# One inference step of a two-layer hybrid trunk: the decode token moved to the second block, the second S5 set-up to the third, and the first retention mixer begun earlier

## The chip, the cores and the metric

The kernel runs on one core of one Trainium2 chip. The metric is the device time of one execution in microseconds (us). The core has five engines that run side by side and meet through semaphores: PE (matrix products; its weight loads are listed apart as PEld), DVE (vector work), ACT (activations, copies), POOL (vector work), and SP, which here only issues DMAs. Each engine works through its own list of instructions in order, so an instruction that waits holds up all that stand behind it on that engine.

## The reference, cut to what matters

A prompt of 2048 tokens and, apart from it, 8 single new tokens with carried states (the decode token below) go through two layers. Each layer is:

```
hn   = rms_norm(x) * norm_w
proj = hn @ w_in                  # 1024 -> 3332 columns
A: RetNet retention on rotated q, k           (4 heads of 64)
B: HGRN2 gated linear recurrence              (4 heads of 64)
C: S5 diagonal complex state space, then GLU  (16 groups, 64 states)
D: Mamba-2 SSD with a causal convolution      (4 heads of 64)
x    = x + concat(A, B, C, D) @ w_out
```

After the second layer a last rms_norm gives y_prompt and y_sample. The states after the prompt and after the decode token are outputs too. All is float32.

## The kernel before

The prompt is cut into four blocks of 512 tokens for each layer, so there are eight blocks, 0 to 3 in the first layer and 4 to 7 in the second. For each block the code runs projections on PE: `gemm_A` (columns of the retention), `gemm_H` (HGRN), `gemm_M` (Mamba) and `gemm_S` (S5), and one block later `out_proj`. Every product is made as three products of high and low parts of its operands; ACT (lines L607, L680) and DVE (L608, L681) split each weight tile first. In the trace the projections are L620, L625 and L687 (L687 with `mx` as its input is `out_proj`).

The work that is no projection is written as generators, the streams, and each `yield` is a place where others may step in. After each piece of a projection `tick()` lets at most two streams of the lanes m, s, a, h (the mixers of the block) and one of the lanes d, e, f, p (decode and set-up) make one step. So the order on PE is the order in which this code runs; the order on the other engines is made by a scheduler that takes the priorities (`SPRI`, `DPRI` and others) into account. `finish(B)` first drains all streams of block B, then runs its `out_proj`.

Three pieces of side work matter here:

- The decode token (class `Dec`). Its 8 rows ride along with the projections of one block of each layer: `dec_pass` multiplies the raw weight tile by them (L630, L694 on PE), `collect` adds the four partial sums (L779 on ACT, L781 on DVE). Its four small mixers (`mix_A`, `mix_H`, `mix_M`, `mix_S` of `Dec`) and `mix_all` are streams. Before, it goes with block 0 and with block 4. `split_T` (L800) turns its normed rows.
- The S5 set-up (`s5_setup`), once for each layer: on DVE powers of the complex decay (`cmul`, `exp_poly`, `sincos`), then tables that pass through HBM (`gpad`, `s5c`: L508, L512, L517, L518) and come back in the S5 mixer (L241, L1447, L1448). The first layer's begins at block 0; the second's, before, at the end of block 1.
- The mixers of a block. For blocks 1 to 7 the mixers A and H begin with the `out_proj` of the block ahead. For block 0 there is none, so before both begin after `gemm_H`, with waits of at most one tick (`most=1`).

Scratch comes from pools of tiles that are handed out again when free: `half` has 10 tiles of 512 columns, `big` 10 of 1024.

Of the kernel before, what the change touches and what calls it, by code (L numbers as in the profile page):

```python
# [113 lines left out]
def trunk_kernel(ctx: ExitStack, tc: tile.TileContext, A: dict):  # L114
# [229 lines left out]
    def sincos(sn, cn, hi, lo, shape):  # L344
        n = tmp_c(shape)
        r = tmp_c(shape)
# [19 lines left out]
    def s5_setup(L):  # L366
# [303 lines left out]
    def gemm_wide(lhs, w, c0, evac, dec=None):  # L670
# [4 lines left out]
        def load(kt):  # L675
            with tc.high_priority(offset=WPRI):
                hl = whp.tile([P, 2, 520], F32R, name=nm("wh"), tag="wh")
                raw = wrp.tile([P, 520], F32, name=nm("wr"), tag="wr")
                nc.sync.dma_start(raw[:, 0:512], w[kt * P : (kt + 1) * P, c0 : c0 + 512])
# [5 lines left out]
        def t_pass(kt, tt):  # L685
            for pi, (a, c) in enumerate(((1, 0), (0, 1), (0, 0))):
                T.matmul(banks[tt], lhs[kt][:, a, tt * P : (tt + 1) * P], hls[kt][:, c, 0:512],  # L687
                         start=(kt == 0 and pi == 0), stop=(kt == KT - 1 and pi == 2))

        def dec_pass(kt):  # L690
            if dec is not None and kt % DW == DW - 1:
                for k in range(kt - DW + 1, kt + 1):
                    j = k % 4
                    T.matmul(dbank[32 * j : 32 * j + 8, :], dec[0]()[:, k, :], raws[k][:, 0:512], start=(k < 4), stop=(k >= 4))  # L694
# [43 lines left out]
    class Blk:  # L738
# [3 lines left out]
        used = 0  # L742

        def free(self, kt):
            return lambda: self.prev is None or self.prev.used > kt
# [41 lines left out]
    class Dec:  # L787
# [209 lines left out]
        def mix_S(self):  # L997
            l, L = self.l, self.L
            gw = load_gw(L)
# [30 lines left out]
            y = half([P, 8, 2, 16])[0:8]  # L1030
# [11 lines left out]
            so = half([P, 2, P])[0:64]  # L1042
# [4 lines left out]
            db = half([P, 2, 256])[0:8]  # L1047
            us = half([P, 2, 256])[0:8]
            nc.sync.dma_start(us[:, 0], self.d["su"])
            nc.sync.dma_start(us[:, 1], self.d["sg"])  # L1050
            nc.sync.dma_start(db[:, 0], A["s5_D"][l].partition_broadcast(8))
            nc.sync.dma_start(db[:, 1], A["s5_glu_b"][l].partition_broadcast(8))
            V.tensor_tensor(db[:, 0], db[:, 0], us[:, 0], ALU.mult)
            V.tensor_tensor(yf, yf, db[:, 0], ALU.add)
# [6 lines left out]
            V.tensor_copy(gT, ps[:, 0:16].rearrange("p (k b) -> p k b", k=2))  # L1061
            yield 4
# [3 lines left out]
            V.tensor_tensor(db[:, 1], db[:, 1], ps[0:8, 0:256], ALU.add)  # L1066
            S.activation(db[:, 1], db[:, 1], AF.Sigmoid)
            V.tensor_tensor(yf, yf, db[:, 1], ALU.mult)
            V.tensor_tensor(yf, yf, us[:, 1], ALU.mult)
# [190 lines left out]
    def mix_H(L, B):  # L1260
# [17 lines left out]
        for l in range(7):  # L1278
            h = 1 << l
            nb = TB // (2 * h)  # L1280
            ntot = (half([P, 2, nb]) if l < 3 else small([P, 2, nb], f"h_t{l}", bufs=1))
# [372 lines left out]
    def out_proj(L, B, src, dst, last, parts=(0, 1)):  # L1654
        w = A["w_out"][L.l]
        fwb = [None, None]
        if last:
# [68 lines left out]
        if not final:  # L1726
            for hf in parts:
                for k, _ in enumerate(gemm_wide(B.mix, w, hf * 512, evac_wide(hf), dec=B.dec and B.dec.out(hf, last))):
                    if hf == 1:
                        B.used = k + 1 if k < 6 else (6 if k == 6 else 8)  # L1730
                    yield
        else:
            gens = []
            for hf in range(4):
                if hf % 2 == 0:
                    dec = B.dec and B.dec.out(hf // 2, last)
                gens.append(gemm(B.mix, w, hf * 256, "T", evac(hf), dec=dec, late=hf == 3))
# [5 lines left out]
            drain(B.st["m"])  # L1743
            for g in gens:
# [110 lines left out]
    for i in range(nblk):  # L1855
# [7 lines left out]
        B.hn, B.st = [], {}  # L1863
# [19 lines left out]
    def begin(ph, B):  # L1883
        B.st[ph] = spawn(ph, mixer(ph, B), most=1 if B.prev is None and ph in "ah" else 9)
# [121 lines left out]
```

## Time and profile before

| what | value |
|---|---|
| three timed runs | 2296.26, 2297.53, 2297.86 us; median 2297.53 |
| the profiled execution | 2296.06 us |
| its span, first to last instruction | 2294.3 us |
| PE busy | 2140.4 us (93%) |
| DVE busy | 1668.9 us (73%) |
| ACT busy | 1037.3 us (45%) |
| POOL busy | 236.4 us (10%) |
| mean granted clock of PE | 0.965 |

Busy time is time in which at least one instruction of the engine runs. A matrix product that runs while the granted clock is 0.5 takes longer and counts as busy for longer, so busy time on PE holds the time that a low clock costs. Rows of waits say which instruction of which line waited for which producer, with the total, the count and the longest.

### The profile page before, as it was taken

To read this page: it belongs to the slowest core of one execution; us is meant where nothing else is said; L and a number is where in the kernel's file an instruction comes from. 1 tells how busy PE (TensorE), PEld (TensorE's weight loads), DVE (VectorE), ACT (ScalarE), POOL (GpSimd) and SP (SyncE) were. 2 spreads that over 40 slices of the span, in tenths; PEclk is the share of its full clock that TensorE was granted. 3 is DMA by queue.
4 is the path that set the end of the run, shared out by engine and by line. 5 is a ranking of instruction groups with operands and counts; after the bars stand their busy time and mean duration, and the time that the engine had idled before them with its cause. 6 is when DMAs were issued, how large, how long until landed. Compare 5 with 4: busy or idle time off the path is not lost. (4 is left out here: it accounts for less than half of the span.)

```text
span 2294.3 us, 41082 instructions
## 1 busy us (share of the span) xinstructions
PE 2140.4 (93%) x15047; PEld 1732.4 (76%) x15047; DVE 1668.9 (73%) x4625; ACT 1037.3 (45%) x1893; POOL 236.4 (10%) x212
## 2 busy tenths in 40 slices
PE   7988898999999999999999999899999989999967
PEld 6767676778777887779777777676877778778856
DVE  6778885587957876397676798658875787647855
ACT  5334633346442464434543365334545345444423
POOL 1010102001022011101020000200101001110100
PEclk9998899999999999999999999999999999999988
DMA  6322466154533655243434246415454433533342
GB/s 190 91 58 71 155 167 155 50 147 127 168 101 109 159 161 165 68 138 87 146 116 134 82 134 180 145 61 177 116 159 122 127 105 100 163 87 109 121 134 84
DMA packets 265242, 284.94 MB, mean 124 GB/s; under 512 B 88848, under 2 KB 185760, under 8 KB 265040
## 3 DMA queue, kind: packets, MB, share of 16 engines
q1 hardware_dynamic: 265040, 282.31, 41.7%
q8 instruction: 118, 1.93, 0.3%
q14 instruction: 84, 0.69, 0.1%
HBM read 246.05 MB, written 31.99 MB: 121 GB/s over the span
## 5 line engine op out<-in xcount | busy, mean ns | idle before, releaser
L687 PE MATMUL gb<-wh,hn 128*128 128x512 f32 x2208 | 542.0, 401 | 3.7 <-DVE half L1626 3.6
L625 PE MATMUL gb<-hn,wh 128*128 128x512 f32 x1920 | 489.0, 408 | 7.0 <-DVE half L1118 7.0
L687 PEld LDWEIGHTS gb<-wh,hn 128*128 128x128 f32 x2208 | 411.3, 189 | 109.8 <-issue 13.8
L625 PEld LDWEIGHTS gb<-hn,wh 128*128 128x128 f32 x1920 | 361.7, 193 | 98.0 <-issue 11.9
L681 DVE TENSOR_TENSOR wh<-wr,wh 128x512 fp32r<-128x512 f32 x296 | 216.3, 735 | 273.2 <-ACT wh L680 271.7
L680 ACT CAST wh<-wr 128x512 fp32r<-128x512 f32 x296 | 183.4, 620 | 394.1 <-PE gb L687 193.4
L687 PE MATMUL gb<-wh,mx 128*128 128x512 f32 x1344 | 339.3, 405 | 7.4 <-DVE half L1700 6.9
L687 PEld LDWEIGHTS gb<-wh,mx 128*128 128x128 f32 x1344 | 250.0, 191 | 75.6 <-DVE half L1700 11.6
L607 ACT CAST wh<-wr 128x512 fp32r<-128x512 f32 (+1 forms) x248 | 152.2, 619 | 320.1 <-PE gb L625 95.9
L608 DVE TENSOR_TENSOR wh<-wr,wh 128x512 fp32r<-128x512 f32 (+1 forms) x248 | 183.2, 745 | 87.0 <-ACT wh L607 85.8
L620 PE MATMUL gb<-wh,hn 128*128 128x256 f32 (+1 forms) x1728 | 225.2, 291 | 2.1 <-DVE hn L556 1.1
L620 PEld LDWEIGHTS gb<-wh,hn 128*128 128x128 f32 x1728 | 217.6, 196 | 5.6 <-issue 2.6
L1561 POOL TENSOR_TENSOR half<-mats,m_lal 128x512 fp32r<-128x512 f32 x64 | 75.4, 1199 | 820.8 <-DVE m_lal L1555 311.0
L1317 DVE COPY_PREDICATED big<-lvl,mb 64x256 f32<-64x256 int32 x192 | 95.9, 538 | 2.7
L1284 ACT COPY zbH<-big 64x512 f32<-64x512 f32 x112 | 70.8, 632 | 46.7 <-PE mb L1293 39.4
L1499 DVE SCALAR_TENSOR_TENSOR big<-gb,vt,big 128x511 f32<-128x511 f32 (+2 forms) x96 | 71.1, 744 | 3.9 <-ACT big L1497 3.4
L1293 PE MATMUL mb<-zbH,big 128*64 128x64 f32 x1536 | 58.2, 232 | 5.2 <-ACT half L1165 3.5
L1293 PEld LDWEIGHTS mb<-zbH,big 128*64 128x64 f32 x1536 | 51.9, 145 | 14.5 <-issue 7.7
L1275 POOL TENSOR_TENSOR big<-mats,h_dg 128x1024 f32<-128x1024 f32 x16 | 30.6, 1932 | 282.3 <-DVE h_dg L1272 282.3
L1458 PE MATMUL mb<-big,big 128*64 128x128 f32 x512 | 40.7, 304 | 18.2 <-DMA big<-s5c 14.2
L620 PE MATMUL gb<-wh,mx 128*128 128x256 f32 x384 | 51.1, 298 | 4.6 <-DVE mx L1481 4.1
L620 PEld LDWEIGHTS gb<-wh,mx 128*128 128x128 f32 x384 | 50.0, 204 | 6.1 <-DVE mx L1481 4.9
(495 smaller groups left out, 3084.6 us busy)
## 6 DMA issues: line engine op xcount, KB each, us to landing
wr<-in_w_in SPq DMA_DIRECT2D x416, 256.0 KB
wr<-in_w_out SPq DMA_DIRECT2D x128, 256.0 KB
big<-s5c SPq DMA_DIRECT2D x64, 256.0 KB
xn<-xmid SPq DMA_DIRECT2D x32, 512.0 KB
xn<-in_x_prompt SPq DMA_DIRECT2D x24, 512.0 KB
big<-s5c SPq DMA_DIRECT2D x24, 512.0 KB
xmid<-half SPq DMA_DIRECT2D x44, 256.0 KB
half<-xmid SPq DMA_DIRECT2D x44, 256.0 KB
```

Of the source, the lines that this page charges most:

```text
L607: S.copy(hl[:, 0, :, :n], raw[:, :, :n])
L608: V.tensor_tensor(hl[:, 1, :, :n], raw[:, :, :n], hl[:, 0, :, :n].bitcast(F32), ALU.subtract)
L620: T.matmul(o, lhs[2 * ks[ki] + k][:, a, tt * P : (tt + 1) * P], hls[ki][:, c, k, :n], start=(ki == 0 and k == 0 and pi == 0 and tt % per = ...
L625: T.matmul(banks[i], hls[ki][:, a, k, i * P : (i + 1) * P], lhs[2 * ks[ki] + k][:, c, :], start=(ki == 0 and k == 0 and pi == 0), stop=(ki ...
L680: S.copy(hl[:, 0, 0:512], raw[:, 0:512])
L681: V.tensor_tensor(hl[:, 1, 0:512], raw[:, 0:512], hl[:, 0, 0:512].bitcast(F32), ALU.subtract)
L687: T.matmul(banks[tt], lhs[kt][:, a, tt * P : (tt + 1) * P], hls[kt][:, c, 0:512], start=(kt == 0 and pi == 0), stop=(kt == KT - 1 and pi = ...
L1284: S.copy(qz[sl, r, :].rearrange("p (b h) -> p b h", h=h), q[sl].rearrange("p a (b two h) -> p (a b) two h", two=2, h=h)[:, :, 1, :])
L1293: T.matmul(ps[su, j * 64 : (j + 1) * 64], k[:, j // 4, (j % 4) * P + 64 * u : (j % 4) * P + 64 * u + 64], qz[:, :, j * 64 + 32 * u : j * 6 ...
L1317: V.copy_predicated(stv[p][su, :, nu * u : nu * u + nu, :], mv, ps[su, p * 256 : p * 256 + 256].rearrange("p (c b h) -> p c b h", c=8, h=h))
L1499: V.scalar_tensor_tensor(acc[:, 3 - i :], ps[:, : TB - 3 + i], w(i), acc[:, 3 - i :], ALU.mult, ALU.add)
L1561: E('m').tensor_tensor(mms[tt][i].rearrange("p (h t) -> p h t", h=4), tri[:, None, :].to_broadcast([P, 4, P]), lal[:, i, tt, :][:, :, None ...
```

## The change

The decode token now goes with block 1 and block 5 (`if B.b == 0: nxt.dec = Dec(...)`), the set-up of the second layer waits until the decode token's S5 mixer is done and so runs in block 2, and block 0's retention mixer begins ahead of `gemm_H`, its HGRN mixer after it (waits of at most two ticks). Beside these the code needs fewer `half` tiles: `cmul` uses its outputs as scratch, several pairs of small tiles share one tile, the GLU weight of the decode token and the final norm weight are loaded later. `ks`, `B.order`, `B.used` and `tmp` are passed through with values that leave the old order of the products.

```diff
     def cmul(outr, outi, ar, ai, br, bi, shape, neg_i=False):
...
-        t1, t2 = tmp_c(shape), tmp_c(shape)
-        V.tensor_tensor(t1, ar, br, ALU.mult)
+        t2 = tmp_c(shape)
+        V.tensor_tensor(outr, ar, br, ALU.mult)
         e.tensor_tensor(t2, ai, bi, ALU.mult)
-        V.tensor_tensor(outr, t1, t2, ALU.subtract)
-        t3, t4 = tmp_c(shape), tmp_c(shape)
+        V.tensor_tensor(outr, outr, t2, ALU.subtract)
+        t3, t4 = outi, tmp_c(shape)
...
-            ctz = half([P, 2, 4, 2, 16])
-            gtile = half([P, 2, 8, 16])
+            cg = half()
+            ctz = cg[:, 0:256].rearrange("p (a q r c) -> p a q r c", a=2, q=4, r=2)
+            gtile = cg[:, 256:512].rearrange("p (z g c) -> p z g c", z=2, g=8)
...
+            if l == 0:
+                ntot = half([P, 2, nb])
+            elif l < 3:
+                if l == 1:
+                    t12 = half([P, 384])
+                ntot = (t12[:, 0:256] if l == 1 else t12[:, 256:384]).rearrange("p (a b) -> p a b", a=2)
...
     def begin(ph, B):
-        B.st[ph] = spawn(ph, mixer(ph, B), most=1 if B.prev is None and ph in "ah" else 9)
+        B.st[ph] = spawn(ph, mixer(ph, B), most=2 if B.prev is None and ph in "ah" else 9)
...
-        B.dec = Dec(layers[0], A["x_sample"].rearrange("b o d -> b (o d)"))
-        ll, dn, ga = load_layer(layers[0]), B.dec.norm(), gemm_A(B.L, B)
+        ll, ga = load_layer(layers[0]), gemm_A(B.L, B)
...
-        next(dn)
-        next(ga)
-        for _ in dn:
-            pass
+        load = setup = None
         setup = spawn("p", s5_setup(layers[0]), SPRI, "s")
...
             run(ga if i == 0 else gemm_A(B.L, B))
+            if B.prev is None:
+                begin("a", B)
             run(gemm_H(B.L, B))
             if B.prev is not None:
-                finish(B.prev, ("a", B), ("h", B), parts=(0, 1) if nxt is not None else (0,))
+                finish(B.prev, ("a", B), ("h", B))
             else:
-                begin("a", B)
                 begin("h", B)
...
+            if B.b == 0:
+                drain(load)
+                nxt.dec = Dec(B.L, B.prev.dec_dst if B.prev else A["x_sample"].rearrange("b o d -> b (o d)"))
+                prep = spawn("d", nxt.dec.norm(), DPRI, "d")
...
             if B.b == 1 and B.l + 1 < DEPTH:
-                    drain(setup)
-                    setup = spawn("p", then(load_layer(layers[B.l + 1]), s5_setup(layers[B.l + 1])), SPRI, "s")
+                load = spawn("p", load_layer(layers[B.l + 1]), SPRI, "s")
+                def after(B):
+                    yield lambda: B.st["ds"].done
+                    yield from s5_setup(layers[B.l + 1])
+                setup = spawn("p", after(B), SPRI, "s")
```

On PE, at block 0's retention mixer (L1163 turns q and k, L1173 scores, L1186 state, L1202 the part from the state; L1270 is the HGRN mixer's first product, L465 the set-up's), there stands before, within `gemm_M`:

```order
L1186 MATMUL mb_1560<-big_744,half_701 64x64 x4
L1202 MATMUL mb_1569<-hAb_111,half_1524 128x128 x2
L1163 MATMUL mb_1572<-mats,half_423 128x128 x2
L1163 MATMUL mb_1572<-mats,half_701 128x128 x2
L1270 MATMUL mb_1579<-mats,big_1527 128x2 x8
L465 MATMUL mb_1597<-s_dm_1462,mats 128x16
L625 MATMUL gb_1498<-hn_147,wh_1602 128x512 x3
```

and now, within `gemm_H`:

```order
L1186 MATMUL mb_1037<-big_652,half_627 64x64 x4
L1202 MATMUL mb_1046<-hAb_111,half_992 128x128 x2
L1163 MATMUL mb_1049<-mats,half_400 128x128 x2
L1163 MATMUL mb_1049<-mats,half_627 128x128 x2
L625 MATMUL gb_967<-hn_149,wh_1060 128x512 x3
L625 MATMUL gb_967<-hn_150,wh_1060 128x512 x3
L625 MATMUL gb_968<-hn_149,wh_1060 128x512 x3
```

The retention's steps moved one projection ahead, and the HGRN mixer's steps no longer stand between them.

On SP, the loads and stores of the first set-up's tables (`gpad` to `s5c`, L517 and L518) and the S5 mixer's loads of them (L1447, L1448) stand before among the loads of rotary tables (L1142) and weights:

```order
L517 DMA big_3423<-gpad_1601 128x8x16 x5
L1447 DMA big_3896<-s5c_2_129 128x512
L604 DMA wr_4099<-in_w_in 128x2x256
L1448 DMA big_3897<-s5c_4_131 128x512
L1142 DMA half_3823<-in_c_rot 128x512
L518 DMA s5c_3_130<-big_3423 128x1024
L1448 DMA big_3897<-s5c_5_132 128x512
L679 DMA wr_4141<-in_w_in 128x512
L1142 DMA half_3838<-in_c_rot 128x512
L1447 DMA big_3896<-s5c_3_130 128x512
```

and now:

```order
L512 DMA s5c_5_132<-big_2676 256x1x128 x4
L517 DMA big_2859<-gpad_1630 128x8x16 x8
L518 DMA s5c_2_129<-big_2859 128x1024
L679 DMA wr_3047<-in_w_in 128x512
L679 DMA wr_3052<-in_w_in 128x512
L679 DMA wr_3159<-in_w_in 128x512
L679 DMA wr_3199<-in_w_in 128x512
L517 DMA big_2869<-gpad_1630 128x8x16 x8
L518 DMA s5c_3_130<-big_2869 128x1024
```

The second store L518 now stands ten rows ahead of the first load of what these stores wrote; before it stood between those loads.

On PE, at the end of block 1's `gemm_M` and the start of its last projection (`gemm_S`'s second half, L625), there stands before:

```order
L620 MATMUL gb_5616<-wh_5740,hn_3008 128x256 x3
L1567 MATMUL mb_5785<-m_la_5667,mats 128x16 x3
L625 MATMUL gb_5799<-hn_2827,wh_5801 128x512 x3
L625 MATMUL gb_5800<-hn_2827,wh_5801 128x512 x3
L625 MATMUL gb_5799<-hn_2835,wh_5801 128x512 x3
L625 MATMUL gb_5800<-hn_2835,wh_5801 128x512 x3
L581 MATMUL mb_5818<-mats,xn_5775 128x128 x4
```

and now (L1574 is L1567 of before):

```order
L630 MATMUL mb_5238<-wr_5391,dT_1792 8x256 x2
L1574 MATMUL mb_5445<-m_la_5289,mats 128x16 x3
L898 MATMUL mb_5458<-half_5304,mats 128x64
L625 MATMUL gb_5467<-hn_2397,wh_5470 128x512 x3
L625 MATMUL gb_5468<-hn_2397,wh_5470 128x512 x3
L625 MATMUL gb_5467<-hn_2405,wh_5470 128x512 x3
L625 MATMUL gb_5468<-hn_2405,wh_5470 128x512 x3
L581 MATMUL mb_5487<-mats,xn_5435 128x128 x4
```

The decode token's products (L630, and L898 of its retention mixer) came into block 1, between products that stood there alone.

## Rows read from the trace of the kernel before

**Rows 1.** The page: busy time by engine, and the granted clock in 40 slices.

```profile
PE 2140.4 (93%) x15047; PEld 1732.4 (76%) x15047; DVE 1668.9 (73%) x4625; ACT 1037.3 (45%) x1893; POOL 236.4 (10%) x212
...
PEclk9998899999999999999999999999999999999988
```

**Rows 2.** Windows: stretch, its length, busy time by engine (instructions), PEclk, DMA share, GB/s.

```profile
0.00:78.00 78.00, 61.04 (x378) 51.56 (x378) 58.74 (x241) 37.88 (x86) 9.93 (x23) 0.96 0.51 156
78.00:129.00 51.00, 51.00 (x250) 36.85 (x247) 28.64 (x100) 22.45 (x44) 2.38 (x1) 1.00 0.33 99
129.00:278.00 149.00, 123.56 (x1044) 100.72 (x1042) 128.00 (x363) 68.74 (x116) 17.88 (x16) 0.87 0.30 89
278.00:346.00 68.00, 64.62 (x395) 50.67 (x394) 59.28 (x163) 28.89 (x64) 10.73 (x8) 0.95 0.63 171
346.00:417.00 71.00, 60.00 (x349) 45.36 (x347) 41.11 (x81) 30.72 (x50) 11.22 (x10) 0.93 0.48 124
417.00:491.00 74.00, 70.25 (x597) 53.37 (x596) 55.49 (x158) 24.83 (x44) 3.77 (x2) 1.00 0.34 104
491.00:766.00 275.00, 262.82 (x1818) 215.42 (x1818) 213.44 (x650) 124.72 (x222) 36.34 (x33) 0.98 0.44 128
766.00:1024.00 258.00, 253.09 (x1757) 207.95 (x1756) 177.57 (x470) 121.63 (x214) 26.67 (x22) 0.99 0.49 137
1024.00:1289.00 265.00, 261.98 (x1850) 207.47 (x1849) 191.17 (x482) 123.46 (x218) 25.57 (x25) 0.99 0.39 119
1289.00:1581.00 292.00, 275.28 (x1956) 214.57 (x1958) 225.94 (x594) 134.54 (x250) 25.91 (x21) 0.98 0.42 125
1581.00:1843.00 262.00, 252.66 (x1764) 206.83 (x1757) 188.96 (x508) 126.75 (x231) 26.22 (x21) 0.99 0.46 138
```

**Rows 3.** Timeline of PE around the decode token's first product: start, us, instruction [idle before].

```profile
33.72 1.02 PE L800 MATMUL mb<-mats,big 8*128 8x8 f32 x8 [4.49 <-DVE big L812]
34.67 5.20 PE L620 MATMUL gb<-wh,hn 128*128 128x256 f32 x24
```

**Rows 4.** Waits of PE from 129 to 278 us: total, times, longest.

```profile
PE mb L722 <- DVE half L736: 9.0, 2, 4.9
PE mb L1186 <- DVE big L1502: 3.9, 1, 3.9
PE mb L1173 <- DVE big L1317: 2.6, 1, 2.6
```

**Rows 5.** Waits of PE from 278 to 417 us.

```profile
PE mb L1458 <- DMA big<-s5c: 8.6, 3, 4.0
PE mb L1474 <- DMA half<-in_s_glu_w: 2.4, 1, 2.4
```

**Rows 6.** Groups of DVE from 129 to 278 us: count | busy us, mean ns | idle before.

```profile
L781 DVE TENSOR_TENSOR half<-half,mb 8x256 f32<-8x256 f32 (+2 forms) x18 | 8.3, 462 | 0.6
...
L1192 DVE SCALAR_TENSOR_TENSOR hAb<-hAb,mats,mb 64x64 f32<-64x64 f32 x16 | 4.5, 278 | 0.3
...
L859 DVE TENSOR_TENSOR half<-half,half 8x512 f32<-8x512 f32 x4 | 3.3, 816 | 0.0
L1176 DVE TENSOR_TENSOR half<-mb,mats 128x256 f32<-128x256 f32 x8 | 3.1, 418 | 0.3 <-PE mb L1173 0.2
...
L735 DVE TENSOR_TENSOR half<-mb,big 128x512 f32<-128x512 f32 x4 | 2.8, 688 | 0.1
...
L858 DVE TENSOR_TENSOR half<-half,half 8x512 f32<-8x512 f32 x4 | 2.6, 672 | 0.0
```

**Rows 7.** Groups of PE over the whole span: the decode token's products.

```profile
L630 PE MATMUL mb<-wr,dT 128*8 128x256 f32 (+1 forms) x256 | 19.6, 381 | 0.0
L694 PE MATMUL mb<-wr,dT 128*8 128x512 f32 x144 | 18.8, 595 | 0.0
```

**Rows 8.** Windows of 40 us in which the DMA engines were busiest.

```profile
760.00:800.00 40.00, 40.00 (x312) 33.35 (x311) 33.30 (x84) 18.20 (x31) 0.00 (x0) 1.00 0.82 183
1360.00:1400.00 40.00, 37.63 (x240) 28.65 (x239) 38.61 (x79) 23.97 (x45) 4.84 (x4) 0.96 0.78 250
```

More of the change, by code (lines that the diff above doesn't have):

```diff
@@ L741, in trunk_kernel @@
         hdone = False
-        used = 0
+        order = tuple(range(KT))
         def free(self, kt):
-            return lambda: self.prev is None or self.prev.used > kt
+            return lambda: self.prev is None or kt in self.prev.used
     def dram(shape, name):
@@ L1029, in mix_S @@
             yield 8
-            y = half([P, 8, 2, 16])[0:8]
+            yso = half()
+            y = yso[0:8, 0:256].rearrange("b (q r c) -> b q r c", q=8, r=2)
             for r in range(2):
@@ L1280, in mix_H @@
             nb = TB // (2 * h)
-            ntot = (half([P, 2, nb]) if l < 3 else small([P, 2, nb], f"h_t{l}", bufs=1))
+            if l == 0:
[4 more added lines that the diff above has]
+                ntot = (t12[:, 0:256] if l == 1 else t12[:, 256:384]).rearrange("p (a b) -> p a b", a=2)
+            else:
+                ntot = small([P, 2, nb], f"h_t{l}", bufs=1)
             qz = zbH
@@ L1656, in out_proj, with load_fw @@
         fwb = [None, None]
-        if last:
+        def load_fw():
             for i in range(2):
@@ L1726, in out_proj @@
         if not final:
+            if last and 1 in parts:
+                load_fw()
             for hf in parts:
-                for k, _ in enumerate(gemm_wide(B.mix, w, hf * 512, evac_wide(hf), dec=B.dec and B.dec.out(hf, last))):
-                    if hf == 1:
-                        B.used = k + 1 if k < 6 else (6 if k == 6 else 8)
+                ks = B.order if hf == 1 else Blk.order
+                for k, _ in enumerate(gemm_wide(B.mix, w, hf * 512, evac_wide(hf), dec=B.dec and B.dec.out(hf, last), ks=ks)):
+                    if hf == 1 and k != 6:
+                        B.used.update(ks[: k + 1])
                     yield
@@ L1862, in trunk_kernel @@
         blocks.append(B)
-        B.hn, B.st = [], {}
+        B.hn, B.st, B.used = [], {}, set()
     def mixer(ph, B):
@@ L1934, in trunk_kernel @@
             nxt = blocks[i + 1] if i + 1 < nblk else None
[L1935 to L1967 removed]
+            if nxt is None:
+                run(gemm_A(B.L, B))
+                run(gemm_H(B.L, B))
+                finish(B.prev, ("a", B), ("h", B), parts=(0,))
                 run(gemm_S(B.L, B))
@@ L1973, in trunk_kernel @@
                 finish(B)
+                break
+            run(ga if i == 0 else gemm_A(B.L, B))
+            if B.prev is None:
+                begin("a", B)
+            run(gemm_H(B.L, B))
+            if B.prev is not None:
+                finish(B.prev, ("a", B), ("h", B))
+            else:
+                begin("h", B)
+            if B.b == 0:
+                convc = zeroed(small([P, 3, 4], "convc"))
+            rows, rs = norm_stats(nxt.b, srcdst(nxt.l)[0])
+            if B.b == 0:
+                drain(load)
+                nxt.dec = Dec(B.L, B.prev.dec_dst if B.prev else A["x_sample"].rearrange("b o d -> b (o d)"))
+                prep = spawn("d", nxt.dec.norm(), DPRI, "d")
+            run(gemm_M(B.L, B))
+            begin("m", B)
+            if B.dec:
+                begin_dec(B, "ahm")
+            if B.b == 0:
+                drain(prep)
+            if nxt.l != B.l:
+                drain(load)
+            norm = norm_block(layers[nxt.l], rows, rs, nxt.hn)
+            run(gemm_S(B.L, B), lambda n: next(norm, 0) if n >= 3 else None)
+            for _ in norm:
+                pass
+            begin("s", B)
+            if B.dec:
+                begin_dec(B, "s")
+            if B.b == 1 and B.l + 1 < DEPTH:
+                load = spawn("p", load_layer(layers[B.l + 1]), SPRI, "s")
[3 more added lines that the diff above has]
+                setup = spawn("p", after(B), SPRI, "s")
+            nxt.dec_dst = B.dec.dst if B.dec else getattr(B, "dec_dst", None)
 _OUT_NAMES = ["y_prompt", "y_sample", "p_ret", "p_hgrn", "p_s5re", "p_s5im", "p_ssm", "p_conv",
```

72 lines of the change are left out of this document (21 added, 51 removed).

## The prediction

> **What bounds the kernel now.** I read the page first: PE is busy for 93% of the span, DVE for 73%, ACT for 45% [rows 1]. PE's list of work hardly changes, so the time falls only where PE stands idle or runs at the low clock. The page's clock digits show 9 or 8 nearly everywhere, so the losses are pieces, not a state, and the next view has to say where they are. I cut the span by stages (the windows of the ends and starts of projections) and took two numbers from each row: length minus PE busy, and (1 - PEclk) times PE busy, which is what the low clock costs. I call the sum the loss of a stretch. From [rows 2]:
>
> - 0 to 78 us (start): 17.0 idle + 0.04 x 61.0 = 19.4 us.
> - 78 to 129 (block 0, `gemm_H`): none.
> - 129 to 278 (block 0, `gemm_M` and `gemm_S`): 25.4 + 0.13 x 123.6 = 41.5 us.
> - 278 to 417 (block 1's `gemm_A`, `gemm_H` over block 0's S5 mixer): 6.6 + 15.2 = 21.8 us.
> - 417 to 491 (block 0's `out_proj`): 3.8 us.
> - 491 to 766 (block 1, with the second set-up at its end): 12.2 + 5.3 = 17.5 us.
> - 766 to 1024 and 1024 to 1289 (blocks 2 and 3, neither side work): 4.9 + 2.5 = 7.4 and 3.0 + 2.6 = 5.6 us.
> - 1289 to 1581 (block 4, with the decode token): 16.7 + 5.5 = 22.2 us.
> - 1581 to 1843 (block 5): 9.3 + 2.5 = 11.8 us.
>
> The reader should see that block 0 loses 67 us where an ordinary block loses 6 or 7, and why: from 129 to 278 us DVE is busy 128 of 149 us, 86%, against 69% in blocks 2 (177.6 of 258). Third, the waits of that stretch: all the large ones end with DVE, the products that store a head's result (L722) 9.0 us, retention's state (L1186) 3.9 us behind the convolution's last instruction, its scores (L1173) 2.6 us behind the HGRN mixer's [rows 4]. One mixer waits behind another mixer's DVE work. Fourth, from 278 to 417 us PE waits for DMA: 8.6 us for the set-up's tables and 2.4 us for the GLU weight [rows 5].
>
> **The change part by part.**
>
> *Start.* The decode token's first product waits 4.5 us for DVE [rows 3], and the low clock in this stretch costs 2.4 us [rows 2]. Both go, since L800 is no longer there; the rest of the 17.0 us idle, the wait for x and its norm, stays. Ends: -6.9 us and 0, the latter if PE then meets weights that are not yet split. From 78 to 129 us PE loses nothing at all, so weights are ahead of it. I take -6.9.
>
> *Block 0, 129 to 278 us.* From DVE go the decode token's sums (L781, 8.3 us), its convolution (L858 and L859, 5.9) and more besides; to the stretch before go retention's state and scores (4.5 + 3.1) and half of the head work that retention shares with HGRN (L735, 2.8) [rows 6]. That is at least 14.2 + 9.0 = 23.2 us, so DVE has 105 us or less. PE's own work at full clock is 0.87 x 123.6 = 107.5 us and loses the same two pieces. The two engines come out about equal, and DVE no longer has two mixers' chains in one queue. The stretch ahead takes retention without harm: DVE is busy only 28.6 of 51 us there [rows 2]. The HGRN chain, the convolutions and the first set-up still meet, so I do not let the loss fall to an ordinary block's. Ends: the whole loss down to the ordinary 3% (7.4 of 258), -38 us; or only what rests on retention's waits, -12 us. I take 15 us left of 41.5, -26.
>
> *278 to 417 us.* On DVE the decode token's mixers go. On SP the tables' stores and loads no longer alternate with rotary tables and weights, and the last store stands well ahead of the first load. So the 8.6 us for the tables and the low clock behind them (0.07 x 60 = 4.2) mostly go; the GLU weight's 2.4 us need not. Ends: -18 (an ordinary 3% of 139 left) and +5, if PE, arriving some 35 us sooner, outruns the tables. I take -14.
>
> *Blocks 1 and 2.* Block 1 gives the set-up to block 2 and takes the decode token. I price each by the block that has it alone: the decode token 22.2 - 5.6 = 16.6 us over an ordinary block, the set-up 17.5 - 7.4 = 10.1. Block 1 goes from 17.5 to about 5.6 + 16.6 = 22.2, +4.7; block 2 takes +10.1. Nothing pays for it elsewhere in this layer. Their cover: the products of `gemm_M` and `gemm_S`, and DVE with 31% free in block 2; if the cover is gone, see the third rival. The wait added ahead of the set-up (`ds` done) has nothing urgent behind it: the tables are wanted in block 4, more than 250 us later. Ends: +5 (the two fit into what is free) and +40.
>
> *Blocks 4 and 5.* Block 4 loses 16.6 us of loss, block 5 gains them: 0, with ends of -8 and +12, as block 5 has 11.8 us of its own to start from against 5.6 in block 3.
>
> *The rest.* The decode token's products cost the same wherever they stand (19.6 + 18.8 us over both layers [rows 7]); in block 1 the q and k columns go through 512-wide products instead of two 256-wide ones, which changes a microsecond at most. `cmul` issues as many instructions as before, but its second product on DVE now writes where the result goes, so nothing grows but a dependency on the same in-order engine. Fewer `half` tiles can only release waits; I take 0. The final norm weight's two loads come later in the last block, ahead of a projection that runs long enough to hide them: 0, ends -3 and +3.
>
> Sum: -6.9 - 26 - 14 + 4.7 + 10.1 + 0 = -32 us. The profiled execution took 2296.06 us, of which the span is 2294.3; the median of the runs is 1.5 us above it. 2297.5 - 32 = 2266 us. Within this case block 0's term at its small end and the tables' at -8 give -12, block 0's at its large end gives -44: 2253 to 2285.
>
> **The rivals.**
>
> *The HGRN chain bounds block 0 by itself (20%).* For it: the largest L722 wait (4.9 us) and the waits behind L1317 belong to HGRN, and it now runs with `most=2` in `gemm_M`, beside the convolutions, as before. Then only retention's waits go: the other L722 wait 4.1, L1186 3.9, L1173 2.6, that is 10.6, with half of the low clock's 16.1: -18.7 instead of -26; and the S5 tables, behind the same chain, give 0 instead of -14. -6.9 - 18.7 + 14.8 = -11: 2287 us. Against it: DVE falls from 86% of the stretch.
>
> *More than I count (14%).* The stretch from 129 to 278 us falls to the ordinary 3% (-38), the tables' waits too (-18): -6.9 - 38 - 18 + 14.8 = -48: 2249 us.
>
> *The decode token makes blocks 1 and 5 what block 0 was (10%), the slower case.* In block 0 it lay with a set-up; in blocks 1 and 5 it lies with the `out_proj` of the block ahead, its evacuations on DVE and the x that passes through HBM. If its part of each of the two blocks then loses what 129 to 278 us lost, 41.5 instead of 16.6, that is +25 twice: -32 + 50 = +18, 2315 us. It decides once each of these blocks loses about 16 us more than I count. Against it: block 4 has the same neighbours, 225.9 us of DVE in 292 (77%), and lost 22.
>
> *DMA is the new bound in blocks 1 and 5 (4%).* The decode token's states and rows, the weights of `out_proj` and x now load together. Of the two busiest windows, one with the DMA engines at 0.82 lost nothing on PE, one with 0.78, within the decode token's block, lost 2.4 + 1.5 us [rows 8]. At 3.9 us per 40 us over some 280 us the two blocks lose 27 instead of 16.6 each, +21: 2287 us. The Trainium skill, DMA: Bandwidth & Descriptors, "Why small descriptors are slow (HBM only)", speaks for this rival: each packet carries a fixed overhead, so the token's many short rows would hold the engines longer than their bytes say. The trace does not bear it out so far: in the window at 0.82 the engines were busier and PE waited for nothing.
>
> That the change does not do what it says is excluded by the order on PE, where retention and the decode token stand in their new places.
>
> **How the numbers follow.** Forecast 52%, HGRN chain 20%, more 14%, slower 10%, DMA 4%. What a measurement of this kernel can tell from no change is about 0.2%, 4.6 us. The forecast, the second rival and most of the first and fourth lie below 2293: faster 82%. Slower takes the third and a little of the edges, 11%; 7% remain within 0.2%. The range of 2246 to 2298 leaves out the slower case and the lower part of the second rival, together under 2 in 10; its lower end lies just under the second rival's 2249, its upper end between the first rival's 2287 and the third's 2315, where blocks 1 and 2 cost +40 and the tables give nothing (-6.9 - 26 + 40 = +7 is past it).
>
> **What would show it.** Right, step by step: no L800 among the first 78 us and PE at L687 about 7 us sooner; DVE under 80% in block 0's `gemm_M` and `gemm_S`, no wait of L1186 behind L1502 there; the wait of L1458 for `s5c` in block 0 under 3 us; a loss of some 22 us in blocks 1 and 5, 17 in block 2, 6 in block 4. Wrong: waits of 3 us and more in block 0's HGRN products (L1293, L1300, L1328, L722) at a DVE as full as before; a loss over 35 us in block 1 or in block 5; or PE waiting for weights (`wr`) there.

## The result, and the profile after

The changed kernel takes 2265.7 us (median of four runs, 2261.5 to 2275.3) against 2296.9 us, a ratio of 0.987 with a 95% interval of 0.984 to 0.991. In a second group of runs the ratio was 0.986 (0.983 to 0.989). The forecast was 2266.

The page of the profile after, busy time by engine and the granted clock in 40 slices, answers to [rows 1]. From the HGRN mixer on, line numbers after the change stand 7 to 9 higher than before: L1300 is what L1293 was, L1465 was L1458, L1509 was L1502, L1709 was L1700.

```profile
PE 2123.5 (94%) x15031; PEld 1719.9 (76%) x15031; DVE 1666.9 (74%) x4622; ACT 1030.6 (46%) x1887; POOL 240.9 (11%) x212
...
PEclk9999999999989999999999999999999999999978
```

DVE does as much as before. The dip of the clock in the fourth and fifth slice (172 to 287 us) is gone; one slice of it stands in the twelfth (622 to 678 us). The windows by stage, with columns as in [rows 2]:

```profile
0.00:66.00 66.00, 52.85 (x322) 46.93 (x322) 47.67 (x190) 33.04 (x72) 10.33 (x23) 1.00 0.63 201
66.00:130.00 64.00, 59.50 (x365) 47.70 (x366) 48.36 (x178) 29.86 (x58) 5.07 (x5) 0.95 0.35 90
130.00:221.00 91.00, 86.74 (x731) 76.24 (x729) 75.78 (x212) 49.90 (x87) 15.63 (x14) 0.98 0.36 99
221.00:290.00 69.00, 67.25 (x482) 50.89 (x482) 53.11 (x160) 27.80 (x57) 6.05 (x6) 0.98 0.60 161
290.00:349.00 59.00, 58.06 (x324) 42.09 (x320) 36.88 (x58) 28.76 (x44) 12.41 (x9) 1.00 0.37 114
349.00:417.00 68.00, 65.46 (x567) 52.44 (x564) 54.02 (x155) 26.06 (x49) 3.77 (x2) 1.00 0.40 124
417.00:638.00 221.00, 204.15 (x1366) 160.10 (x1364) 180.56 (x504) 109.64 (x202) 23.47 (x19) 0.98 0.44 130
638.00:727.00 89.00, 76.73 (x612) 58.21 (x612) 70.77 (x257) 26.43 (x48) 3.77 (x2) 0.92 0.31 98
727.00:998.00 271.00, 261.69 (x1803) 215.12 (x1801) 196.54 (x500) 122.36 (x216) 39.06 (x34) 0.97 0.49 138
998.00:1254.00 256.00, 251.69 (x1759) 206.73 (x1758) 176.75 (x467) 121.72 (x214) 28.20 (x25) 0.99 0.42 126
1254.00:1517.00 263.00, 259.31 (x1848) 206.82 (x1846) 186.48 (x472) 124.45 (x225) 26.96 (x21) 1.00 0.39 121
1517.00:1811.00 294.00, 275.90 (x1954) 215.57 (x1952) 233.32 (x633) 136.00 (x256) 26.35 (x21) 0.98 0.44 132
```

With the prediction's loss (length less PE busy, plus (1 - PEclk) times PE busy):

| stretch | loss before | forecast | loss after |
|---|---|---|---|
| start | 19.4 | 12.5 | 13.1 |
| block 0, `gemm_H` to `gemm_S` | 41.5 | 15 | 7.5 + 6.0 |
| block 1's `gemm_A` and `gemm_H` | 21.8 | 7.8 | 3.1 + 0.9 |
| block 0's `out_proj` | 3.8 | 3.8 | 2.5 |
| block 1 to the end of its `out_proj` | 17.5 | 22.2 | 20.9 + 18.4 |
| block 2 | 7.4 | 17.5 | 17.2 |
| block 3 | 5.6 | 5.6 | 6.8 |
| block 4 | 22.2 | 5.6 | 3.7 |
| block 5 | 11.8 | 28.4 | 23.6 |

The two stretches that follow went from 18.1 + 52.9 to 14.4 + 49.9. All together the loss fell by 34 us, and the span by 34.5. PEclk is printed to two digits, so the loss of a stretch of 260 us is good to some 1.3 us. So time came from block 0 as forecast, some 6 us more of it; block 1's output projection took some 14 us that were not forecast.

### The profile page after: what moved, and what is told of

It reads as the page before. It is cut to its first block, busy times and chain, and to the rows that moved or that the text cites. A ratio compares the mean times of both kernels' runs of the same rounds, so it can differ in the third digit from the quotient of the medians.

```text
span 2259.8 us, 41047 instructions
## 1 busy us (share of the span) xinstructions
PE 2123.5 (94%) x15031; PEld 1719.9 (76%) x15031; DVE 1666.9 (74%) x4622; ACT 1030.6 (46%) x1887; POOL 240.9 (11%) x212
## 5 line engine op out<-in xcount | busy, mean ns | idle before, releaser
L687 PE MATMUL gb<-wh,hn 128*128 128x512 f32 x2208 | 542.7, 401 | 5.3 <-DVE half L1633 1.8
L687 PEld LDWEIGHTS gb<-wh,hn 128*128 128x128 f32 x2208 | 410.9, 188 | 108.3 <-issue 9.6
L625 PE MATMUL gb<-hn,wh 128*128 128x512 f32 x1920 | 481.5, 404 | 11.5 <-DVE half L1118 5.4
L625 PEld LDWEIGHTS gb<-hn,wh 128*128 128x128 f32 x1920 | 357.6, 191 | 98.5 <-issue 10.1
L687 PE MATMUL gb<-wh,mx 128*128 128x512 f32 x1344 | 341.7, 407 | 8.1 <-DVE half L1709 7.8
L687 PEld LDWEIGHTS gb<-wh,mx 128*128 128x128 f32 x1344 | 252.5, 193 | 76.5 <-DVE half L1709 14.0
L608 DVE TENSOR_TENSOR wh<-wr,wh 128x512 fp32r<-128x512 f32 (+1 forms) x248 | 185.2, 753 | 76.9 <-ACT wh L607 75.8
L620 PEld LDWEIGHTS gb<-wh,hn 128*128 128x128 f32 x1728 | 215.6, 194 | 11.8 <-issue 8.6
L1291 ACT COPY zbH<-big 64x512 f32<-64x512 f32 x112 | 70.4, 629 | 37.3 <-PE mb L1300 29.4
L1300 PE MATMUL mb<-zbH,big 128*64 128x64 f32 x1536 | 55.6, 226 | 6.6 <-ACT half L1165 3.5
L1300 PEld LDWEIGHTS mb<-zbH,big 128*64 128x64 f32 x1536 | 49.6, 139 | 15.8 <-issue 9.2
L1120 POOL TENSOR_TENSOR half<-half,half 128x256 f32<-128x256 f32 x32 | 32.1, 1003 | 197.4 <-DVE half L1118 176.0
```

Source lines behind the costliest of these rows:

```text
L608: V.tensor_tensor(hl[:, 1, :, :n], raw[:, :, :n], hl[:, 0, :, :n].bitcast(F32), ALU.subtract)
L620: T.matmul(o, lhs[2 * ks[ki] + k][:, a, tt * P : (tt + 1) * P], hls[ki][:, c, k, :n], start=(ki == 0 and k == 0 and pi == 0 and tt % per = ...
L625: T.matmul(banks[i], hls[ki][:, a, k, i * P : (i + 1) * P], lhs[2 * ks[ki] + k][:, c, :], start=(ki == 0 and k == 0 and pi == 0), stop=(ki ...
L687: T.matmul(banks[tt], lhs[ks[kt]][:, a, tt * P : (tt + 1) * P], hls[kt][:, c, 0:512], start=(kt == 0 and pi == 0), stop=(kt == KT - 1 and ...
L1291: S.copy(qz[sl, r, :].rearrange("p (b h) -> p b h", h=h), q[sl].rearrange("p a (b two h) -> p (a b) two h", two=2, h=h)[:, :, 1, :])
L1300: T.matmul(ps[su, j * 64 : (j + 1) * 64], k[:, j // 4, (j % 4) * P + 64 * u : (j % 4) * P + 64 * u + 64], qz[:, :, j * 64 + 32 * u : j * 6 ...
```

## The experiments

Each was timed beside the kernel before. Ratios are to that kernel, with a 95% interval.

### Block 0: which part of the change pays?

**Late retention.** The changed kernel with its early retention undone, place and pace.

```diff
-            if B.prev is None:
-                begin("a", B)
             run(gemm_H(B.L, B))
...
             else:
+                begin("a", B)
                 begin("h", B)
...
-... most=2 if B.prev is None and ph in "ah" else 9)
+... most=1 if B.prev is None and ph in "ah" else 9)
```

> The changed kernel, but with block 0's retention mixer begun after gemm_H again, beside HGRN's, both at the old pace (most=1). The decode token, the second set-up and the scratch tiles stay as changed. My theory (placement and early retention each take work out of VectorE's queue in block 0): retention's waits in gemm_M and gemm_S come back, some 10.6 us and a little low clock, 2278 us (2272 to 2284); the start and the wait for the S5 tables stay cured. Rival, early retention is what does it: 2288 us or more. Rival, the scratch tiles do it, or retention's place is indifferent: 2266 us, within 4.

Measured: 2284.8 us, ratio 0.996 (0.994 to 0.998), just above my range and under the rival's 2288. First its windows from `gemm_H` on, then PE's waits in the second of them:

```profile
66.00:111.00 45.00, 45.00 (x198) 36.34 (x197) 31.26 (x113) 22.70 (x45) 2.40 (x1) 1.00 0.50 127
111.00:247.00 136.00, 113.47 (x994) 97.96 (x993) 108.18 (x313) 57.99 (x101) 21.84 (x19) 0.87 0.25 67
247.00:438.00 191.00, 185.60 (x1277) 141.10 (x1277) 132.30 (x329) 79.86 (x145) 22.01 (x16) 0.99 0.47 137
```

```profile
PE mb L722 <- DVE half L736: 13.5, 2, 8.0
PE mb L1173 <- DVE big L1324: 4.6, 1, 4.6
```

Block 0's `gemm_M` and `gemm_S` lose 37 us, nearly the 41.5 of before, though the token's work on DVE is gone but for its norm. What the token's move cures is the stretch behind it: 247 to 438 us loses 7, where 278 to 491 lost 25.6 before. Moving token and set-up without retention is worth 10 us, the scratch included.

**Early retention only**, on the kernel before: the same edit the other way round.

```diff
+            if B.prev is None:
+                begin("a", B)
             run(gemm_H(B.L, B))
...
-                begin("a", B)
                 begin("h", B)
...
-... most=1 if B.prev is None and ph in "ah" else 9)
+... most=2 if B.prev is None and ph in "ah" else 9)
```

> The kernel before, with one part of the change alone: block 0's retention mixer begins before gemm_H and may take waits of 2. My theory: the 10.6 us of waits that retention has in gemm_M and gemm_S go, the rest of block 0's loss (decode token's first product, HGRN's stores, S5 tables) stays: about 2285 us (2280 to 2290). Rival, retention is what does it: 2275 us or less. Rival, the decode token does it alone: 2297 us, within 4.

Measured: 2297.4 us, ratio 1.001 (1.000 to 1.003): nothing, where I had expected 12 us. Windows, and PE's waits from 258 to 351 us (line numbers as before the change):

```profile
141.00:258.00 117.00, 99.87 (x791) 80.03 (x783) 96.06 (x257) 59.02 (x103) 19.61 (x17) 0.93 0.38 107
258.00:421.00 163.00, 136.93 (x840) 104.51 (x836) 114.43 (x292) 64.39 (x119) 18.43 (x16) 0.92 0.49 130
```

```profile
PE mb L1350 <- DVE half L502: 6.6, 1, 6.6
PE mb L1591 <- DVE half L735: 4.1, 1, 4.1
PE gb L687 <- DVE half L900: 3.3, 1, 3.3
```

The gain is made and given back. With the 1.9 us that `gemm_H` now loses, the first stretch goes from 41.5 to 26, but the next goes from 21.8 to 37: the HGRN mixer now ends there (L1350), behind the first set-up (L502) and the decode token (L900).

**Scratch only**: the kernel before with the smaller scratch of the change, and nothing else.

```diff
-        t1, t2 = tmp_c(shape), tmp_c(shape)
-        V.tensor_tensor(t1, ar, br, ALU.mult)
+        t2 = tmp_c(shape)
+        V.tensor_tensor(outr, ar, br, ALU.mult)
...
+            cg = half()
+            ctz = cg[:, 0:256].rearrange("p (a q r c) -> p a q r c", a=2, q=4, r=2)
...
```

> The kernel before, with the smaller scratch alone: cmul without two of its four temporaries, shared half tiles in the set-up, in the decode token's S5 mixer and in the HGRN mixer; the later load of the decode token's GLU weight is part of it. My theory: no wait in the trace of before ends with a half tile coming free, so 2297 us, within 4. Rival, VectorE and SyncE wait for half tiles behind other waits, and the change's gain is these tiles: 2280 us or less.

Measured: 2290.6 us, ratio 0.998 (0.997 to 1.000). Between none and 8 us; the rival's 17 is out.

**Early place, old pace.** The changed kernel with one number set back, so that only the place of retention is left of its part.

```diff
-... most=2 if B.prev is None and ph in "ah" else 9)
+... most=1 if B.prev is None and ph in "ah" else 9)
```

> The changed kernel with block 0's retention and HGRN mixers at the old pace (most=1 instead of 2), retention still begun beneath gemm_H. It parts the place of the retention mixer from its pace, which the run with late retention undid together. My theory (the place decides, since it takes retention's VectorE work out of gemm_M and gemm_S): the changed kernel's time, 2261 to 2267 us. Rival, the pace decides (waits of 2 let the projections' own VectorE work go ahead): 2278 us or more, as with late retention.

Measured: 2293.9 us, ratio 0.998 (0.997 to 1.000). My theory falls, and the rival's 2278 or more stands: with the pace set back nearly the whole gain is gone, and the early place by itself is no better than late retention (0.996). The window of `gemm_M` and `gemm_S`:

```profile
133.00:256.00 123.00, 102.00 (x825) 88.53 (x823) 93.82 (x256) 53.81 (x95) 20.59 (x15) 0.88 0.29 76
```

DVE is at 76% here, less than in the changed kernel (75.8 of 91 us, 83%), and PE loses 33 us. So a full DVE is not what binds. The HGRN mixer's steps on PE show what does. First this kernel's timeline, then the changed kernel's (start, us, instruction [idle before]):

```profile
145.67 1.15 PE L1300 MATMUL mb<-zbH,big 128*64 128x64 f32 x32
...
152.95 1.97 PE L1300 MATMUL mb<-zbH,big 128*64 128x64 f32 x32 [3.16 <-DVE big L1324]
...
163.38 1.98 PE L1300 MATMUL mb<-zbH,big 128*64 128x64 f32 x32 [3.75 <-ACT zbH L1291]
...
186.40 3.42 PE L1307 MATMUL mb<-zbH,big 128*64 128x128 f32 x16 [2.38 <-ACT zbH L1291]
...
228.47 0.69 PE L722 MATMUL mb<-mats,half 128*128 128x128 f32 x2 [8.34 <-DVE half L736]
```

```profile
146.19 1.15 PE L1300 MATMUL mb<-zbH,big 128*64 128x64 f32 x32
...
154.56 1.15 PE L1300 MATMUL mb<-zbH,big 128*64 128x64 f32 x32 [0.67 <-ACT wh L607]
...
165.88 1.81 PE L1300 MATMUL mb<-zbH,big 128*64 128x64 f32 x32
...
198.51 1.96 PE L1307 MATMUL mb<-zbH,big 128*64 128x128 f32 x16
```

Each step of the chain needs a result that DVE and ACT make from the step before. At pace 1 the next step stands one piece of a projection behind; PE reaches it before that result is there and stands still. At pace 2 there are two pieces in between, and the wait is filled. The chain takes longer (L1307 at 198.5 instead of 186.4 us), and PE loses nothing by it. Late retention with pace 2 was not run, so it is not shown whether the early place is needed beside the pace.

**Without the decode token**, the changed kernel and the kernel before. In both it is left out altogether.

```diff
-                nxt.dec = Dec(B.L, B.prev.dec_dst if B.prev else A["x_sample"].rearrange("b o d -> b (o d)"))
-                prep = spawn("d", nxt.dec.norm(), DPRI, "d")
...
-                    yield lambda: B.st["ds"].done
```

> The changed kernel with the decode token left out altogether (its products, mixers, states and outputs), the second set-up not waiting for it. It prices the token where it now stands. My theory: some 19 us of products in each layer's blocks at TensorE's low end of 39 us for both, and 15 + 17 us of loss in blocks 1 and 5: 2266 - 39 - 32 = 2195 us (2185 to 2210). Rival, the token's mixers now lie beside work that hides them, and only the products go: 2227 us. Rival, the loss of blocks 1 and 5 belongs to something else there: 2220 us or more with their losses above 15 us.

> The kernel before with the decode token left out altogether (its products, mixers, states and outputs), to stand against the changed kernel without it (2164 us). In block 0 the two then differ by the place and pace of the retention mixer and by the scratch tiles. My theory (early retention pays once the token's work is off VectorE's queue, by whatever means): retention is worth some 20 us here, 2184 us (2178 to 2192), and the 129 to 278 us stretch still loses 25 us or more. Rival, retention pays little and the token alone made block 0's loss: 2168 us, within 4. Rival, the token costs the same in both places: 2297 - 97 = 2200 us or more.

Measured: 2163.9 us (0.943, 0.940 to 0.946) and 2182.3 us (0.951, 0.948 to 0.954). The first is outside my range and below both rivals, the second within its range. The token costs 97 us after the change and 112 before: more than the 71 that I had put together from its products and the loss of its blocks, since 72 of the 97 are busy time of PE (2123.5 with it, 2051.8 without), not 39. By these differences its new place is worth 15 us, and without it retention (place and pace) and scratch are worth 18; both come from kernels timed in different groups and are good to some 10 us. The window of `gemm_M` and `gemm_S` in the kernel before without the token, and the same in the changed one without it:

```profile
110.50:241.00 130.50, 108.24 (x980) 94.22 (x979) 104.32 (x303) 52.49 (x94) 19.88 (x19) 0.91 0.28 76
```

```profile
129.50:217.00 87.50, 81.29 (x659) 71.91 (x659) 67.39 (x175) 45.30 (x81) 14.76 (x13) 0.98 0.41 109
```

32 us of loss against 8 (15 with the `gemm_H` that now holds retention): most of the 41.5 us that this stretch lost before is there without the token too. The losses side by side:

| kernel | retention | pace | token in block 0 | `gemm_H` to `gemm_S` | up to the end of block 0's `out_proj` |
|---|---|---|---|---|---|
| before | late | 1 | yes | 41.5 | 25.6 |
| early retention only | early | 2 | yes | 26.0 | 40.9 |
| late retention | late | 1 | no | 37.3 | 7.3 |
| early place, old pace | early | 1 | no | 43.3 | 6.8 |
| the change | early | 2 | no | 13.5 | 7.1 |

### Block 1's output projection: 14 us that were not forecast

In the changed kernel PE waits there in retention's mixer: the product with the state (L1202) stands until DVE has masked the scores (L1176). PE's waits from 638 to 727 us, and DVE's timeline just ahead of the one that ends the first:

```profile
PE mb L1202 <- DVE half L1176: 5.4, 1, 5.4
PE gb L687 <- DVE half L1709: 1.4, 1, 1.4
```

```profile
651.78 0.40 DVE L435 COPY pwr<-half 128x16 f32<-128x16 f32 x4
...
653.10 0.68 DVE L298 TENSOR_TENSOR big<-pwr,bb 128x512 f32<-128x512 f32 x1
...
654.02 0.69 DVE L302 TENSOR_TENSOR big<-pwr,bb 128x512 f32<-128x512 f32 x1
654.63 0.75 DVE L1176 TENSOR_TENSOR half<-mb,mats 128x256 f32<-128x256 f32 x2
```

L298, L302 and L435 are the second set-up, some hundred small instructions in one piece, ahead of L1176 in an in-order queue: the scores (L1173) are through on PE at 649.3 us, L1176 begins at 654.63. Five kernels move or cut that piece.

**Later**, after block 1's output projection:

```diff
-                    yield lambda: B.st["ds"].done
+                    yield lambda: B.st["ds"].done and len(B.used) == KT
```

> The changed kernel, but the second S5 set-up starts only when block 1's output projection is through, some 85 us later. In the changed kernel PE lost 18.4 us in 638 to 727 us, where the set-up's hundred small VectorE instructions stand ahead of the mixers' (5.4 us of it in one wait of L1202). My theory (the in-order queue of VectorE, at a place where retention and HGRN start): that stretch loses 3 to 6 us, block 2 some 20 instead of 17, so about 2256 us (2252 to 2260). Rival, the loss belongs to the set-up and goes where it goes: 2266 us, within 4, and the stretch of block 2 loses 30. Rival, the stretch's loss belongs to the output projection beside the mixers: 638 to 727 us keeps 15 us or more and the time is 2266 us or above.

Measured: 2278.5 us, ratio 0.992 (0.989 to 0.994), by the ratios 10 to 13 us more than the change (its interval overlaps that of the 0.987 a little). The projection's loss fell to 6 us, but block 2 lost 38 instead of 17. The longest wait there, from 720 to 770 us, ends with ACT:

```profile
PE mb L1357 <- ACT half L1337: 12.9, 1, 12.9
```

ACT's timeline shows why: the HGRN mixer's L1337, whose input PE had finished at 735.1 us (L1335), stands behind the set-up's own steps on ACT (L359, L363), and these wait for the piece on DVE:

```profile
747.83 0.21 ACT L359 ACTIVATE half<-cm_s 128x8 f32<-128x8 f32 x1 [7.80 <-DVE cm_s L358]
...
751.16 1.05 ACT L1337 COPY half<-mb 128x512 f32<-128x512 f32 x2
```

The rival had the mechanism, that the loss goes where the set-up goes, but not the size: it forecast no change in time and a loss of 30.

The next two kernels were measured beside the changed kernel itself, run again:

> The changed kernel once more, as the measure for the others of this group: 2266 us, within 6; a ratio to the kernel before between 0.984 and 0.991.

Measured: 2260.9 us, ratio 0.986 (0.983 to 0.989).

**One block later:**

```diff
-                def after(B):
-                    yield lambda: B.st["ds"].done
-                    yield from s5_setup(layers[B.l + 1])
-                setup = spawn("p", after(B), SPRI, "s")
+            if B.b == 2 and B.l + 1 < DEPTH:
+                setup = spawn("p", s5_setup(layers[B.l + 1]), SPRI, "s")
```

> The changed kernel, but the second S5 set-up starts when block 2's four projections have been issued, one block later, so that its hundred small VectorE instructions fall into block 3's gemm_A, beside no retention and no HGRN mixer; that is the neighbour they had in the kernel before. My theory (the set-up costs what its neighbours on VectorE's queue lose): the 18.4 us of block 1's output projection fall to 3 to 5, block 2 to 7, block 3 rises from 7 to 17: 16 us less than the changed kernel measured beside it (10 to 20 less), about 2250 us. Rival, the set-up costs some 25 us in any place that is not block 1's gemm_A: the time of the changed kernel, within 4.

Measured: 2269.3 us, ratio 0.989 (0.986 to 0.992). The expected gain did not come; the time is 8 us above the changed kernel beside it. The projection's loss fell to 7.5 us, and the next stretch lost 33. In it, one wait:

```profile
PE mb L1615 <- DVE half L1602: 16.5, 1, 16.5
```

I had looked only for retention and HGRN as neighbours. The Mamba mixer's L1602 stands behind the piece here (L303 is the set-up's):

```profile
833.46 0.28 DVE L303 TENSOR_TENSOR half<-half,half 128x128 f32<-128x128 f32 x1
...
836.00 0.68 DVE L1602 TENSOR_TENSOR half<-half,half 128x512 f32<-128x512 f32 x1
```

**In pieces**, seven times between the set-up's first parts:

```diff
+        if l:
+            yield 3
```

> The changed kernel, but the first part of the second set-up, which was issued in one piece of some hundred VectorE instructions, is cut into eight pieces with waits of 3 between them, so that other work is issued in between. My theory (one mixer waits behind the whole piece in an in-order queue): the wait of 5.4 us at L1202 goes, and 638 to 727 us loses about 10 instead of 18.4: 8 us less than the changed kernel (3 to 12 less). Rival, VectorE has too much work in this stretch as a whole (70.8 of 89 us): no less than the changed kernel, within 3.

Measured: 2262.8 us, ratio 0.986 (0.983 to 0.989), the same as the change, as the rival had it. The wait of L1202 is gone (the longest left there is 3.8 us, at the HGRN mixer's L1300), and the two windows that hold the set-up lose 11 + 15 us instead of 18 + 17:

```profile
645.60:727.50 81.90, 73.55 (x603) 55.33 (x601) 63.31 (x190) 24.66 (x45) 3.77 (x2) 0.96 0.32 99
727.50:998.30 270.80, 260.82 (x1819) 214.44 (x1812) 204.43 (x554) 123.57 (x221) 38.79 (x34) 0.98 0.52 141
```

The 9 us that the trace gains here do not show in the time: the same execution loses 12 us more than the changed kernel's in its other stretches.

**One block and five steps later:**

```diff
+                def after(B):
+                    yield 5
+                    yield from s5_setup(layers[B.l + 1])
-                setup = spawn("p", s5_setup(layers[B.l + 1]), SPRI, "s")
+                setup = spawn("p", after(B), SPRI, "s")
```

> As the run with the second set-up one block later, but begun five steps of the projections later still, so that the SSM mixer's L1602, which waited 16.5 us behind the set-up's first instructions, stands ahead of them in VectorE's queue. My theory (the set-up costs what the one mixer step behind its dense piece loses): block 2 and 3's stretch loses 17 to 20 us instead of 33, the time is 10 to 14 us under the changed kernel, about 2250 us. Rival, the set-up's VectorE work costs 25 us in any place: as the run one block later, 2265 to 2270 us.

Measured: 2258.8 us, ratio 0.985 (0.982 to 0.987), between theory and rival. The place is as expected: no wait of L1615, and the windows lose 4 + 16 us, where the kernel five steps earlier lost 7.5 + 33 and the changed one 18 + 17.

```profile
642.00:716.50 74.50, 70.25 (x600) 53.38 (x602) 55.13 (x162) 24.29 (x43) 3.77 (x2) 1.00 0.33 104
716.50:990.00 273.50, 262.68 (x1820) 215.04 (x1812) 215.13 (x633) 122.44 (x218) 36.97 (x35) 0.98 0.45 130
```

On DVE the set-up begins at 811 us here and at 809 in the kernel five steps earlier: what differs is which mixer's step stands behind it in the queue. So the set-up costs 9 us over an ordinary block in one place, near the 10 that it cost before, and, counted the same way over 4 and 7 us for the two windows, 24 to 33 in three others; cut in pieces, 15. It is the fastest kernel here, but by its time it can't be told from the change (0.986 and 0.987), beside which it was not run. Of the 15 us that its trace gains in this stretch some 11 are lost elsewhere in the same execution, in stretches whose work on PE is the same: 25 instead of 21 us in block 1, 10 instead of 4 in block 4, all of it low clock. Why, stays open.

**Not after the token**: the set-up may start where it did before, with two buffers for what the token still reads.

```diff
-                    yield lambda: B.st["ds"].done
...
-        L.abr, L.abi = ltile([P, 8], "abr"), ltile([P, 8], "abi")
+        L.abr, L.abi = ltile([P, 8], "abr", bufs=2), ltile([P, 8], "abi", bufs=2)
```

(and the same for `bb` and `ct`)

> The changed kernel, but the second set-up does not wait for the decode token's S5 mixer: the layer's four small S5 constants have two buffers, so it may begin where it did in the kernel before, during block 2's gemm_A. My theory (the wait for the token moved the set-up's dense piece in front of retention's and HGRN's first steps): 638 to 727 us loses 4 to 7 instead of 18.4, the stretch before it some 26 instead of 21, together 8 to 12 us less than the changed kernel: about 2252 us. Rival, with the token there VectorE is full and the loss only changes place: 2260 to 2267 us.

Measured: 2274.5 us, ratio 0.992 (0.989 to 0.995), by the ratios 10 to 13 us more than the change and above the rival too. The projection's loss falls to 10, and the stretch ahead of it rises to 46. From 514 to 600 us:

```profile
PE mb L1005 <- DMA half<-in_state_s_re: 16.0, 1, 16.0
```

The token's S5 mixer now waits for its state, whose load is late: SP issues it at 579.7 us, in the changed kernel at 533.9. In SP's list it now stands behind the set-up's loads (L437, L438) and its first table store (L398). Whether these or the set-up's `half` tiles hold it up was not tried.

## Why the prediction was right, and where its reasons failed

- **Sum and start.** Loss fell by 34 us, forecast 32. No token stands in the first 66 us, and PE reaches L687 at 43.3 us instead of 53.6, part of which is the token's products that no longer stand there. The loss of the start fell by 6.3 us, forecast 6.9.
- **Block 0's `gemm_M` and `gemm_S`: right in size, wrong in cause.** Forecast -26, measured -28. The working took 23.2 us of work off DVE and said that PE's losses follow. Three kernels contradict it. With the token gone the stretch lost 37 us, with token and retention gone from it 33, at DVE 76%, and in the kernel before without any token 32, at DVE 80%. Only where the pace goes from 1 to 2 does it fall. The step that failed is "The two engines come out about equal, and DVE no longer has two mixers' chains in one queue": the loss did not hang on how much DVE had to do. The number that counted stands in the first rival, that the HGRN mixer runs "with `most=2` in `gemm_M`, beside the convolutions, as before": it was taken for a side matter, and with the early place it was the part that paid: with it alone set back the stretch loses 43 us instead of 13.5. The rival's mechanism, a chain of steps on which PE waits by itself, was the true one; its price assumed that the chain can't be spread. The sign that I had named, DVE under 80%, was of no use: it is 83% in the changed kernel and 76% in the one that loses, since a stretch that loses less is also shorter. The other sign held: no wait of 3 us in 130 to 221 us, where the longest are these:

```profile
PE gb L620 <- DVE big L1509: 2.9, 2, 1.5
PE mb L1300 <- ACT wh L607: 0.7, 1, 0.7
```

- **The terms do not add.** I priced retention and token apart and summed. Alone, early retention at pace 2 gives 0 (2297.4 us), moved token and set-up with the scratch 10; together they give 31 to 35. With pace 2 HGRN's end comes to lie in block 1's `gemm_A`; where the token's and the set-up's steps stood there too (early retention only), the next stretch lost what the first had gained (15 us each).
- **The tables.** Forecast -14, measured -17.8. No wait for `s5c` is left in block 0, as named; [rows 5] had 8.6 us. It is the token's move that does it: with late retention the stretch is as good.
- **Blocks 1 and 5, the token.** Forecast 16.6 us over an ordinary block. Block 1 before its `out_proj` lost 20.9 and block 5 lost 23.6, near the 22 named as a sign. The sum itself had 28.4 for block 5, since it added the 16.6 to what block 5 lost already; the two did not agree.
- **Block 1's output projection: missed.** Block 1 lost 39 us in all, past the 35 that I had called wrong. The failed step: "The wait added ahead of the set-up (`ds` done) has nothing urgent behind it". True of the tables, but the wait also moves a dense piece of DVE work from block 2's `gemm_A` to the first steps of retention and HGRN. The price of 10.1 us for the set-up was read at a place where nothing urgent stood behind it, and holds in such a place only: 9 us in one, 24 and more in three others. Block 2 lost 17.2 us, as forecast (17.5), but not for the whole set-up.
- **Why the sum held.** Block 1's miss of +17 was paid by the tables (-4), blocks 4 and 5 (-7), the end (-7) and block 0's small surplus. Terms that err by 17 and by 7 gave a total within 2 us. That the forecast of 2266 came so near is luck.
- **The other rivals.** DMA was no bound: PE has no wait for weights in blocks 1 and 5, neither for `wr` nor for the split tiles `wh`; its waits for DMA there, for `s5c`, are 3.6 and 1.7 us. The slower case did not come: blocks 1 and 5 did not become what block 0 was, because block 0's large loss in `gemm_M` and `gemm_S` was not the token's.

## What to carry to other kernels

Where PE waits on a chain of another engine, count the pieces of other work that stand between two steps of the chain before you count the work on the engine that ends the waits: the busy share of DVE ranked these kernels wrongly. The price of a dense piece of many small instructions in an in-order queue hangs on which steps stand behind it (9 to 33 us here, with single waits of up to 16.5), so it is read from the place the piece will have, not from where it stood. And parts of a change that move a wait on to the next stretch are priced together: one was worth 0, the other 10, both 31 to 35.

## What the runs showed of the hardware that was not expected

The low clock does not cost the same in every execution. Up to 640 us the changed kernel and the one with the set-up after block 1's output projection have the same instructions on PE in the same order, and up to 624 us on DVE too. In block 1 the one was granted 0.98 (the window of 417 to 638 us above), the other 0.95:

```profile
419.00:643.00 224.00, 208.23 (x1361) 163.42 (x1359) 174.02 (x457) 108.96 (x201) 22.85 (x19) 0.95 0.43 128
```

So the low level (half of full speed) cost 4 us against 10 out of some 206 us of work. In a second execution of the changed kernel itself it cost 6. The clock took back most of the 15 us that one trace above had gained; of the 12 us that the trace in pieces lost again it took less than half. And a wait costs more than its length: after the wait of 3.16 us in the timeline above the same 32 products took 1.97 us instead of 1.15.
